# ConvFFN of a two-layer backbone: partial sums of the seven products kept in PSUM, copied out by ScalarE

## The chip, the core and the metric

The kernel runs on one core of a Trainium2 chip. Its engines have queues of their own: TensorE (PE in the profile, its weight loads PEld), VectorE (DVE), ScalarE (ACT), GpSimd (POOL) and SyncE (SP), which here issues nearly all DMAs. The metric is the device time of one execution in microseconds (us).

## The reference, cut to what matters

Two layers work on 1024 latent tokens of width 1024; the first also updates 256 context tokens. Both layers end in this feed-forward network, in float32:

```python
def conv_ffn(h, w_up, conv_w, conv_b, w_down):      # D_FF = 2816
    a = h @ w_up                                    # (L, 1024) @ (1024, 5632)
    gate, val = a[..., :D_FF], a[..., D_FF:]
    gp = jnp.pad(gate, ((0, 0), (1, 1), (0, 0)))
    g = gp[:, 0:L] * conv_w[0] + gp[:, 1:1 + L] * conv_w[1] + gp[:, 2:2 + L] * conv_w[2] + conv_b
    return (jax.nn.silu(g) * val) @ w_down
...
x = x + g2 * conv_ffn(modulate(x, norm2_g[layer], sh2, sc2), ...)
```

## The kernel before

Everything is transposed: channels lie on the 128 partitions, tokens along the free dimension. A float32 product is made of three TensorE passes over high and low parts (`PASSES`); `split` (L445) makes the parts, the high one with a copy on ACT (L447), the low one with a subtraction on DVE or POOL (L448).

The tokens are worked in two halves, one after the other (`s` = 0, 1), and D_FF in 22 blocks of 128 channels (`f`). A step `up(s, f, ...)` computes the gate and the value of one block for one half. The half's tokens are cut once more into two pieces of n columns, and the 1024 input channels into two parts, so that a step is a 2x2 by 2x2 block product; it is done with seven block products `P1` to `P7` in place of eight (`PROD`), each 12 matmuls of n columns into one PSUM bank. n is 320 and 324 in layer 0 (latents and context), 256 and 258 in layer 1. The results are `c00`, `c01` (the gate's two pieces) and `c10`, `c11` (the value's), in one SBUF tile `hx`:

- `c00` = P1 + P2, `c01` = P1 + P6 + P5 + P3,
- `c10` = P1 + P6 + P7 + P4, `c11` = P1 + P6 + P7 + P5.

Each product has a bank of its own (tag `pq`, eight buffers, all of PSUM). ACT copies P1 out (L323), and seven additions on DVE (`add`, L311) make the four sums. `gate` (L315 to L321) applies the convolution and the silu; L361 multiplies by the value, and a split makes the tile `act`, the moving operand of the down product.

Between the products of step f stand four calls of `down` (L368) for earlier blocks: two blocks' `act` by the weights `wd`, 6 matmuls into a bank (over all 2n columns at n = 256, else two banks of n columns), which a DVE instruction adds to the stream `xl` (L382). A step has 84 matmuls of products and 48 of n columns of `down` (24 of 512 columns at n = 256).

A step's weights are seven operands. Two loads of 512 KB, SP's `load0` (gate columns, tile `wr`, halves A00 and A01) and `load1` (value columns, A10 and A11), are combined on POOL: S1 = A10 + A11 (L241), S3 = A00 - A10 (L247, over A10), S2 = S1 - A00 (L248, over A00), S4 = A01 - S2 (L251, over S1). Each of A00, S2, S1, S4 (tiles `wh`), A01, S3, A11 (`wq`) is then split into its slot, which can be written when PE has done the product that uses it: A00 by P1, A01 by P2, S2 by P6, S1 by P5, S3 by P7, A11 by P4, S4 by P3. In most steps POOL makes the low parts of A00, A01 and A11, DVE the others. There are two `wr` buffers, so the next `load0` waits until S2 is split and S4 made, the next `load1` until S3 and A11 are split. All of this runs two steps ahead of the products.

`ORDER` is the order in which a step's products are written; `FEED` says after which product which weight is split, `AFTER` after which product how many `down` calls stand; `todo` lists the additions with the products that each needs. The order that the engines really get is set by a scheduler when the program is built; instructions written under `high_priority` are preferred by it.

Of the kernel before, what the change touches and what calls it, by code (L numbers as in the profile page):

```python
# [11 lines left out]
AF = mybir.ActivationFunctionType  # L12
# [3 lines left out]
P = 128  # L16
# [62 lines left out]
class Ffn:  # L79
# [10 lines left out]
                P6=("S2", "T2"), P7=("S3", "T3"))  # L90
# [1 line left out]

    ORDER = ("P1", "P2", "P6", "P5", "P7", "P4", "P3")
    FEED = dict(P2=("A00",), P6=("A01",), P5=("S2",), P7=("S1", "load0"), P4=("S3", "A11", "load1"), P3=("S4", "s"))
    AFTER = dict(P5=1, P4=1, P3=2)
    AFTER2 = dict(P4=1, P3=3)

    ORDER0 = ("P1", "P2", "P3", "P5", "P6", "P7", "P4")
# [175 lines left out]
    def up(self, s, f, hooks, downs, prep, beside):  # L274

        nc, net = self.nc, self.net
        h = self.halves[s]
        n = h.n
        g0 = s * NF + f
        self.busy = len(downs) > 0  # L280
        if g0 == 0:
            now, w = self.first
            self.slots["A11"] = self.t([P, 2, 4, P], "wq", F32R, 3)
            self.soon = self.up_weights(1, self.slots)
            self.soon["load0"]()
        else:
            w = self.slots
        soon = self.soon if g0 + 1 < 2 * NF else {}
        steps = dict(soon) if g0 + 1 < 2 * NF else {}
        for x in ("load0", "load1", "s"):  # L290
            steps.pop(x, None)
        if g0 + 2 < 2 * NF:
            self.soon = self.up_weights((f + 2) % NF, self.slots)
            steps.update((x, self.soon[x]) for x in ("load0", "load1", "s"))
        gv = net.t(net.hpool, [P, net.width], "hx", bufs=2)
        C0, C1 = gv[:, :2 * n], gv[:, self.w2:self.w2 + 2 * n]
        c00, c01, c10, c11 = C0[:, :n], C0[:, n:], C1[:, :n], C1[:, n:]
        cw, layer = net.convw[self.layer], self.layer
        g = self.t([P, self.w2], "g", bufs=1)[:, :2 * n]

        def product(p):
            wn, bn = self.PROD[p]
            o = net.t(net.ps, [P, 512], "pq" if p in ("P2", "P5") else "pq")[:, :n]
            for k in range(4):
                for i, (wp, sp) in enumerate(PASSES):
                    nc.tensor.matmul(o, w[wn][:, wp, k], self.part(s, bn, k, sp), start=(k == 0 and i == 0),  # L306
                                     stop=(k == 3 and i == 2))
            return o

        def add(o, x, y):  # L310
            nc.vector.tensor_tensor(o, x, y, ALU.add)  # L311

        def gate():
            w0, w1, w2 = (cw[:, j * NF + f:j * NF + f + 1] for j in range(3))
            nc.scalar.activation(g, C0, AF.Identity, bias=net.convb[:, layer * NF + f:layer * NF + f + 1], scale=w1)  # L315
            for _, _, m, c in h.span:
                nc.vector.scalar_tensor_tensor(g[:, c + 1:c + m], C0[:, c:c + m - 1], w0, g[:, c + 1:c + m],
                                               ALU.mult, ALU.add)
                nc.vector.scalar_tensor_tensor(g[:, c:c + m - 1], C0[:, c + 1:c + m], w2, g[:, c:c + m - 1],
                                               ALU.mult, ALU.add)  # L320
            nc.scalar.activation(g, g, AF.Silu)  # L321
        x = {}
        todo = [("P1", lambda: nc.scalar.activation(c00, x["P1"], AF.Copy)),  # L323
                ("P1 P6", lambda: add(c10, x["P6"], c00)),
                ("P6 P2", lambda: add(c00, c00, x["P2"])),
                ("P6 P5", lambda: add(c01, x["P5"], c10)),
                ("P6 P5 P7", lambda: add(c10, c10, x["P7"])),
                ("P6 P5 P7", lambda: add(c11, c10, x["P5"])),
                ("P6 P5 P7 P4", lambda: add(c10, c10, x["P4"])),
                ("P6 P5 P3", lambda: add(c01, c01, x["P3"])),  # L330
                ("P6 P5 P3 P2", gate)]
        order, feed = (self.ORDER if f else self.ORDER0, self.FEED if f >= 2 - s else (self.FEED0, self.FEED1)[f])
        cut = 3 - f if f < 2 and s == 0 else 7
        for i, p in enumerate(order):
            if i == cut:
                yield
            x[p] = product(p)
            if g0 == i == 0:
                w["A11"] = self.t([P, 2, 4, P], "wd", F32R, 4)
                for st in (now["A11"], soon["load1"], soon["s"]):  # L340
                    st()
            if i in hooks:
                hooks[i]()
            if i == 2:
                prep()
            if i in beside:
                beside[i]()
            for it in [it for it in todo if set(it[0].split()) <= set(x)]:
                todo.remove(it)
                with net.tc.high_priority():  # L350
                    it[1]()
            m = (self.AFTER if f != 2 else self.AFTER2).get(p, 0)
            for fn in downs[:m]:
                fn()
            downs = downs[m:]
            for st in feed.get(p, ()):
                if st in steps:
                    steps[st]()
        act = self.acts[f] = self.act()
        with net.tc.high_priority():  # L360
            nc.vector.tensor_tensor(g, g, C1, ALU.mult)  # L361
            self.tail = net.split(act[:, 0, :2 * h.n], act[:, 1, :2 * h.n], g)
# [66 lines left out]
class Net:  # L429
# [487 lines left out]
    def fourier(self, fl, fc, tables, pool):  # L917
# [876 lines left out]
```

## Time and profile before

| | |
|---|---|
| time, median of 3 runs | 2914.47 us (2912.04 to 2919.38) |
| the profiled execution | 2920.99 us; its span, from the first to the last instruction, 2919.1 us |
| busy, share of the span | PE 95%, PEld 86%, DVE 76%, ACT 45%, POOL 43% |
| feed-forward network of layer 0 | about 486 to 1440 us of the span |
| feed-forward network of layer 1 | about 2137 to 2919 us |
| products (L306) and down products (L376) | 7392 and 3696 matmuls |
| additions (L311) | 616 |

Times in the profile are from the start of the span. A busy share is an average over stages with different limits, so the two networks, and the two halves in each, are read apart. A group of the profile is the instructions of one line, engine and operation with equal tile names: its count, its busy time, the mean duration of one in ns, and behind the second bar the engine's idle time just before them with what ended it.

### The profile page before, as it was taken

Reading aid. Unit: us, or ns where it says so; the run is one execution under the profiler, and the core shown is the slowest. Engines: PE = TensorE matmul, PEld = TensorE weight load, DVE = VectorE, ACT = ScalarE, POOL = GpSimd, SP = SyncE. Lnnn points to the kernel's source line nnn. Section 1 sums busy time; section 2 is a strip of 40 time slices with the busy share of each in tenths; the row PEclk is TensorE's granted clock in tenths of the full one; section 3 lists DMA queues with packets and bytes.
Section 4 is the critical chain, followed back from the end, with each engine's and each line's share of the span. In section 5 each row is a group of like instructions: output and inputs, shape, how many; then the busy total and the mean of one; then the engine's idle time right before and its main releaser. Section 6 shows DMA issues by size and latency. Waiting matters only on the chain.

```text
span 2919.1 us, 47590 instructions
## 1 busy us (share of the span) xinstructions
PE 2772.8 (95%) x17978; PEld 2522.4 (86%) x17978; DVE 2216.9 (76%) x3748; ACT 1302.0 (45%) x2448; POOL 1267.9 (43%) x1044
## 2 busy tenths in 40 slices
PE   7999998899999999999999998999989999899998
PEld 4668877799999899999888888998778888799998
DVE  4243477999989999998767668996498777887786
ACT  4221314434444443443443336996354444444443
POOL 0600025455555755553311112443455665666663
PEclk9999999899999999999899999999989999999999
DMA  8663262322223222222052327772133323333323
GB/s 303 215 189 118 98 217 72 112 74 86 80 87 101 75 80 87 73 81 87 24 169 101 137 109 183 180 179 80 37 109 101 95 87 98 105 89 93 94 88 95
DMA packets 335886, 327.67 MB, mean 112 GB/s; under 512 B 16217, under 2 KB 264617, under 8 KB 335657
## 3 DMA queue, kind: packets, MB, share of 16 engines
q1 hardware_dynamic: 331509, 315.69, 35.9%
q0 software_dynamic: 3808, 7.87, 0.9%
q8 instruction: 143, 2.34, 0.3%
q10 hardware_dynamic: 340, 1.06, 0.1%
q14 instruction: 86, 0.70, 0.1%
HBM read 277.86 MB, written 46.71 MB: 111 GB/s over the span
## 4 chain that ended last, share of the span: by engine, by line
PE 61%; DVE 14%; DMA 7%; POOL 7%; issue 5%; ACT 5%; SPq 0%; POOLq 0%; DVEq 0%; ACTq 0%
PE pq L306 18%; PE pq L478 15%; PE pq L376 11%; PE ps L478 6%; DMA wr<-in_ffn_w_up_dram 4%; POOL ws L241 2%; DVE xl L382 2%; DVE wh L448 2%; PE pq L566 2%; POOL wh L448 2%; DVE hx L311 2%; PE ps L487 2%; ACT t L1227 1%; POOL wr L248 1%; DMA wd<-in_ada_w_dram 1%
## 5 line engine op out<-in xcount | busy, mean ns | idle before, releaser
L376 PE MATMUL pq<-act,wd 128*128 128x320 f32 (+3 forms) x3696 | 639.8, 322 | 59.3 <-DVE xl L382 24.5
L376 PEld LDWEIGHTS pq<-act,wd 128*128 128x128 f32 x3696 | 557.1, 193 | 92.0 <-DVE xl L382 28.7
L306 PE MATMUL pq<-hs,wh 128*128 128x320 f32 (+3 forms) x4128 | 607.5, 299 | 16.3 <-DVE xl L382 7.8
L306 PEld LDWEIGHTS pq<-hs,wh 128*128 128x128 f32 x4128 | 576.9, 191 | 26.4 <-DVE xl L382 11.2
L306 PE MATMUL pq<-hs,wq 128*128 128x320 f32 (+3 forms) x3144 | 469.8, 299 | 8.4 <-DVE wq L448 4.9
L478 PE MATMUL pq<-hs,wh 128*128 128x512 f32 (+3 forms) x2100 | 469.0, 358 | 3.6 <-DVE hs L724 1.9
L306 PEld LDWEIGHTS pq<-hs,wq 128*128 128x128 f32 x3144 | 442.5, 191 | 14.1 <-DVE wq L448 5.7
L478 PEld LDWEIGHTS pq<-hs,wh 128*128 128x128 f32 x2100 | 365.8, 193 | 78.0 <-issue 6.2
L241 POOL TENSOR_TENSOR ws<-wr 128x512 f32<-128x512 f32 x88 | 153.6, 1745 | 397.3 <-DMA wr<-in_ffn_w_up_dram 333.0
L447 ACT ACTIVATE wh<-wr 128x512 fp32r<-128x512 f32 (+1 forms) x223 | 161.8, 726 | 354.0 <-POOL wr L248 201.5
L382 DVE SCALAR_TENSOR_TENSOR xl<-pq,mod,xl 128x320 f32<-128x320 f32 (+5 forms) x616 | 304.1, 514 | 11.7 <-PE pq L376 11.6
L448 DVE TENSOR_TENSOR wh<-wr,wh 128x512 fp32r<-128x512 f32 (+1 forms) x147 | 166.9, 1135 | 184.8 <-ACT wh L447 184.5
L448 POOL TENSOR_TENSOR wq<-wr,wq 128x512 fp32r<-128x512 f32 x152 | 235.7, 1550 | 32.9 <-ACT wq L447 32.9
L478 PE MATMUL ps<-hs,wh 128*128 128x512 f32 x840 | 240.0, 405 | 3.6 <-ACT hs L721 1.8
L311 DVE TENSOR_TENSOR hx<-hx,pq 128x320 f32<-128x320 f32 (+3 forms) x440 | 196.1, 448 | 29.1 <-PE pq L306 21.6
L447 ACT ACTIVATE wq<-wr 128x512 fp32r<-128x512 f32 x262 | 160.0, 623 | 101.3 <-PE pq L306 73.2
L447 ACT ACTIVATE wh<-ws 128x512 fp32r<-128x512 f32 x172 | 107.5, 625 | 169.8 <-PE pq L306 115.4
L478 PEld LDWEIGHTS ps<-hs,wh 128*128 128x128 f32 x840 | 141.9, 191 | 41.6 <-issue 14.4
L251 POOL TENSOR_TENSOR ws<-wr 128x512 f32<-128x512 f32 x88 | 120.2, 1366 | 123.3 <-DVE wh L448 112.3
L999 POOL TENSOR_TENSOR hsp<-hsq,hsp 128x512 fp32r<-128x512 f32 (+1 forms) x40 | 47.1, 1185 | 265.5 <-ACT hsq L998 265.5
L1006 DVE RECIPROCAL hsq<-hsq 128x512 f32<-128x512 f32 (+1 forms) x40 | 121.1, 3030 | 52.9 <-ACT hsq L1005 52.1
L448 DVE TENSOR_TENSOR wd<-wrd,wd 128x512 fp32r<-128x512 f32 x176 | 155.5, 912 | 0.2 <-ACT wd L447 0.2
(310 smaller groups left out, 4555.5 us busy)
## 6 DMA issues: line engine op xcount, KB each, us to landing
wr<-in_ffn_w_up_dram SPq DMA_DIRECT2D x176, 512.0 KB, 4.4
wrd<-in_ffn_w_down_dram SPq DMA_DIRECT2D x88, 512.0 KB, 3.5
adaw<-in_ada_w_dram SPq DMA_DIRECT2D x128, 256.0 KB, 3.6
wd<-in_ada_w_dram SPq DMA_DIRECT2D x32, 512.0 KB, 5.1
wr<-in_odd_w_qkv_dram SPq DMA_DIRECT2D x24, 512.0 KB, 3.9
vd<-kvs SPq DMA_DIRECT2D x8, 1280.0 KB
v<-vd SPq DMA_DIRECT2D x16, 640.0 KB
kd<-kvs SPq DMA_DIRECT2D x8, 1280.0 KB, 4.6
```

What stands on the lines that cost most here:

```text
L241: op(raw["S1"], raw["A10"], raw["A11"], ALU.add)
L251: op(x, raw["A01"], raw["S2"], ALU.subtract)
L306: nc.tensor.matmul(o, w[wn][:, wp, k], self.part(s, bn, k, sp), start=(k == 0 and i == 0), stop=(k == 3 and i == 2))
L311: nc.vector.tensor_tensor(o, x, y, ALU.add)
L376: nc.tensor.matmul(pd, self.wds[j][i][:, wp, d % 4], self.acts[f][:, sp, lo:lo + m], start=(i == 0 and pi == 0), stop=(i == len(fs) - 1 an ...
L382: nc.vector.scalar_tensor_tensor(x, pd[:, a - lo:b - lo], net.mod[:, self.layer, st, 5, d:d + 1], x, ALU.mult, ALU.add)
L447: self.nc.scalar.activation(h, src, AF.Copy)
L448: return (e or self.nc.vector).tensor_tensor(l, src, f32(h), ALU.subtract)
L478: nc.tensor.matmul(o, w(wp, k), s(k, sp), start=(ki == 0 and pi == 0), stop=(ki == len(order) - 1 and pi == 2))
L487: nc.tensor.matmul(out, l[a], r[b], start=(first and i == 0), stop=(last and i == 2))
L566: nc.tensor.matmul(acc[32 * q:32 * q + 32, 0:256], self.sT[:, k, :], w[q // 2][:, 256 * (q % 2):256 * (q % 2) + 256], start=(k == 0), stop ...
L1006: nc.vector.reciprocal(r, r)
```

## The change

In all steps but f = 0, P6 is accumulated into the bank of P1, P7 further into the same bank, and P3 into the bank of P5; in steps 3 to 20 (`last`) P4 goes into the first bank as well. Between the products ACT copies the bank's state to SBUF: after P1 (`c00`), after P6 (`c01`), after P7 (`c10`), and in steps 3 to 20 after P4 (`c10` again). DVE keeps the additions of P2 to `c00`, of P5 to make `c11`, and of the second bank to `c01`. A step 3 to 20 thus has four copies and three additions in place of one and seven, and uses three banks for its products in place of seven. A product that adds to a bank can't start before the bank has been copied out, and P3 not before the addition that reads P5. One `down` call moves from behind P5 to behind P7 (`AFTER`).

```diff
-    AFTER = dict(P5=1, P4=1, P3=2)
+    AFTER = dict(P7=1, P4=1, P3=2)
...
-            o = net.t(net.ps, [P, 512], "pq" if p in ("P2", "P5") else "pq")[:, :n]
+            o = net.t(net.ps, [P, 512], "pq")[:, :n] if p not in onto else x[onto[p]]
             for k in range(4):
                 for i, (wp, sp) in enumerate(PASSES):
-                    nc.tensor.matmul(o, w[wn][:, wp, k], self.part(s, bn, k, sp), start=(k == 0 and i == 0),
-                                     stop=(k == 3 and i == 2))
+                    nc.tensor.matmul(o, w[wn][:, wp, k], self.part(s, bn, k, sp),
+                                     start=(p not in onto and k == 0 and i == 0),
+                                     stop=(k == 3 and i == 2), skip_group_check=p in onto)
...
+        def copy(o, x):
+            nc.scalar.activation(o, x, AF.Copy)
+        x, onto = {}, {}
+        last = f > 2 and len(downs) > 0
+        if f == 0:
...
+        else:
+            onto = dict(P6="P1", P7="P6", P3="P5")
+            if last:
+                onto["P4"] = "P7"
+            todo = [("P1", lambda: copy(c00, x["P1"])),
+                    ("P2", lambda: add(c00, c00, x["P2"])),
+                    ("P6", lambda: copy(c01, x["P6"])),
+                    ("P7", lambda: copy(c10, x["P7"])),
+                    ("P7", lambda: add(c11, c10, x["P5"])),
+                    ("P4", lambda: copy(c10, x["P4"]) if last else add(c10, c10, x["P4"])),
+                    ("P3", lambda: add(c01, c01, x["P3"])),
+                    ("P3", gate)]
```

Outside the two networks the order of instructions stays as it was. Inside, the scheduler moves more than the additions. (In the new program the copies are L325, the splits L466 and L467, the silu L323, the gate L317; L236, L241, L247, L248, L251, L261 keep their numbers. Numbers behind tile names count buffers.)

ACT in a step of layer 1's second half, before: the high parts of A00, then the copy of P1, the silu, A01, `act`, S1, S2, S3, A11, S4, and the next gate.

```order
L447 ACTIVATE wh_20746<-wr_27112 128x512 [waits DMAHW1_49,PE_49]
L323 ACTIVATE hx_27208<-pq_27210 128x258 [waits PE_49]
L321 ACTIVATE g_27005<-g_27005 128x516 [waits DVE_49,Activation_49]
L447 ACTIVATE wq_20648<-wr_27112 128x512 [waits PE_49]
L447 ACTIVATE act_27204<-g_27005 128x516 [waits DVE_49]
L447 ACTIVATE wh_20747<-ws_27202 128x512 [waits PE_49,Pool_49]
L447 ACTIVATE wh_20746<-wr_27112 128x512 [waits Pool_49]
L447 ACTIVATE wq_20649<-wr_27148 128x512 [waits DMAHW2_49,PE_49]
L447 ACTIVATE wq_20973<-wr_27148 128x512 [waits PE_49]
L447 ACTIVATE wh_20747<-ws_27202 128x512 [waits PE_49,Pool_49]
L315 ACTIVATE g_27209<-hx_27208,cols_31_139,cols_175_786 128x516 [waits DVE_49,Activation_49]
```

The same place now, from S1 on: S1, `act`, the copy of P6, S2 (which waits for POOL's L248), S3, the copy of P7, two splits of `wd`, A11, the copy of P4, S4.

```order
L466 ACTIVATE wh_20543<-ws_27440 128x512 [waits PE_49,Pool_49]
L466 ACTIVATE act_27442<-g_27248 128x516 [waits DVE_49]
L325 ACTIVATE hx_27446<-pq_27448 128x258 [waits PE_49]
L466 ACTIVATE wh_20542<-wr_27352 128x512 [waits Pool_49]
L466 ACTIVATE wq_20445<-wr_27387 128x512 [waits DMAHW3_49,PE_49]
L325 ACTIVATE hx_27446<-pq_27448 128x258 [waits PE_49]
L466 ACTIVATE wd_27691<-wrd_27498 128x512 [waits DMAHW4_49,PE_49]
L466 ACTIVATE wd_27694<-wrd_27498 128x512 [waits PE_49]
L466 ACTIVATE wq_20769<-wr_27387 128x512 [waits PE_49]
L325 ACTIVATE hx_27446<-pq_27448 128x258 [waits DVE_49,PE_49]
L466 ACTIVATE wh_20543<-ws_27440 128x512 [waits PE_49,Pool_49]
```

The copies of P6 and P7 stand behind splits that wait for POOL, and P7 and P4 on PE wait for them; A11 now stands behind P4, which PE reaches only after the copy of P7.

POOL in one step of layer 1's first half, before: S1, S3, the low part of A00, S2, that of A01, S4, that of A11.

```order
L241 TENSOR_TENSOR ws_22846<-wr_22808 128x512 [waits DMAHW1_49,DVE_49]
L247 TENSOR_TENSOR wr_22808<-wr_22780,wr_22808 128x512 [waits DMAHW0_49,Pool_49]
L448 TENSOR_TENSOR wh_20746<-wr_22780,wh_20746 128x512 [waits PE_49,Activation_49]
L248 TENSOR_TENSOR wr_22780<-ws_22846,wr_22780 128x512 [waits Pool_49]
L448 TENSOR_TENSOR wq_20648<-wr_22780,wq_20648 128x512 [waits PE_49,Activation_49]
L251 TENSOR_TENSOR ws_22846<-wr_22780 128x512 [waits DVE_49,Pool_49]
L448 TENSOR_TENSOR wq_20973<-wr_22808,wq_20973 128x512 [waits PE_49,Activation_49]
```

Now the steps go in pairs. From the end of one step's combining through the other's:

```order
L251 TENSOR_TENSOR ws_22761<-wr_22724 128x512 [waits DVE_49,Pool_49]
L467 TENSOR_TENSOR wh_20542<-wr_22864,wh_20542 128x512 [waits DMAHW6_49,PE_49,Activation_49]
L467 TENSOR_TENSOR wq_20444<-wr_22864,wq_20444 128x512 [waits PE_49,Activation_49]
L467 TENSOR_TENSOR wq_20769<-wr_22724,wq_20769 128x512 [waits PE_49,Activation_49]
L241 TENSOR_TENSOR ws_22928<-wr_22891 128x512 [waits DMAHW0_49,DVE_49]
L247 TENSOR_TENSOR wr_22891<-wr_22864,wr_22891 128x512 [waits Pool_49]
L248 TENSOR_TENSOR wr_22864<-ws_22928,wr_22864 128x512 [waits Pool_49]
L251 TENSOR_TENSOR ws_22928<-wr_22891 128x512 [waits DVE_49,Pool_49]
L467 TENSOR_TENSOR wq_20769<-wr_22891,wq_20769 128x512 [waits PE_49,Activation_49]
L467 TENSOR_TENSOR wh_20542<-wr_23031,wh_20542 128x512 [waits DMAHW1_49,PE_49,Activation_49]
L467 TENSOR_TENSOR wq_20444<-wr_23031,wq_20444 128x512 [waits PE_49,Activation_49]
```

A00 and A01 of the next step (from the tile that its `load0` fills) are now split before L241, while `load1` is awaited; in one step of a pair A11 stands in front of them, in the other behind them. In layer 1's second half, and in layer 0's, one step of a pair has A00 and A01 ahead of L241 and the other has one or both between L241 and L248, as before.

SP in the same half, before: `load0`, `load1` one behind the other, then the load of a `wd` pair (`wrd`).

```order
L236 DMA wr_22780<-in_ffn_w_up_dram 128x8x128 [waits DMAHW5_49,Pool_49]
L236 DMA wr_22808<-in_ffn_w_up_dram 128x8x128 [waits DMAHW6_49,DVE_49,Pool_49]
L261 DMA wrd_22904<-in_ffn_w_down_dram 128x2x512 [waits DMAHW7_49,DVE_49]
L236 DMA wr_22952<-in_ffn_w_up_dram 128x8x128 [waits DMAHW0_49,Pool_49]
L236 DMA wr_22980<-in_ffn_w_up_dram 128x8x128 [waits DMAHW1_49,DVE_49,Pool_49]
L261 DMA wrd_23076<-in_ffn_w_down_dram 128x2x512 [waits DMAHW2_49,DVE_49]
```

Now:

```order
L236 DMA wr_22864<-in_ffn_w_up_dram 128x8x128 [waits DMAHW3_49,DVE_49,Pool_49]
L261 DMA wrd_22986<-in_ffn_w_down_dram 128x2x512 [waits DMAHW4_49,DVE_49]
L236 DMA wr_22891<-in_ffn_w_up_dram 128x8x128 [waits DMAHW5_49,Pool_49]
L236 DMA wr_23031<-in_ffn_w_up_dram 128x8x128 [waits DMAHW6_49,DVE_49,Pool_49]
L261 DMA wrd_23153<-in_ffn_w_down_dram 128x2x512 [waits DMAHW7_49,DVE_49]
L236 DMA wr_23058<-in_ffn_w_up_dram 128x8x128 [waits DMAHW0_49,Pool_49]
```

`load0` goes out as soon as S2 is split; `load1` waits for A11 on POOL alone, and the load of `wrd` stands between the two. On PE a step's order is now P1, P2, P5, P6, P7, P4, P3 (before: P1, P2, P6, P5, P7, P4, P3), with `down` matmuls before P6, around P7, and the next P1 begun before P4.

More of the change, by code (lines that the diff above doesn't have):

```diff
@@ L321, in gate @@
             nc.scalar.activation(g, g, AF.Silu)
[L322 to L331, printed above, removed]
+        def copy(o, x):
[4 more added lines that the diff above has]
+            todo = [("P1", lambda: copy(c00, x["P1"])),
+                    ("P1 P6", lambda: add(c10, x["P6"], c00)),
+                    ("P6 P2", lambda: add(c00, c00, x["P2"])),
+                    ("P6 P5", lambda: add(c01, x["P5"], c10)),
+                    ("P6 P5 P7", lambda: add(c10, c10, x["P7"])),
+                    ("P6 P5 P7", lambda: add(c11, c10, x["P5"])),
+                    ("P6 P5 P7 P4", lambda: add(c10, c10, x["P4"])),
+                    ("P6 P5 P3", lambda: add(c01, c01, x["P3"])),
+                    ("P6 P5 P3 P2", gate)]
+        else:
+            onto = dict(P6="P1", P7="P6", P3="P5")
+            if last:
+                onto["P4"] = "P7"
+            todo = [("P1", lambda: copy(c00, x["P1"])),
+                    ("P2", lambda: add(c00, c00, x["P2"])),
[5 more added lines that the diff above has]
+                    ("P3", gate)]
         order, feed = (self.ORDER if f else self.ORDER0, self.FEED if f >= 2 - s else (self.FEED0, self.FEED1)[f])
```

## The prediction

> **What bounds the kernel now.** I read the page's head first, then the engines' busy time by stage, then one row of each stage that gives the length of a step, and last PE's waits and the chain of waits in the stages where PE stands idle.
>
> ```profile
> span 2919.1 us, 47590 instructions
> ...
> PE 2772.8 (95%) x17978; PEld 2522.4 (86%) x17978; DVE 2216.9 (76%) x3748; ACT 1302.0 (45%) x2448; POOL 1267.9 (43%) x1044
> ```
>
> The profiled execution took 2920.99 us, 1.9 more than its span and 6.5 more than the median of the three runs, 2914.47. The sum below is a difference, which I subtract from both. All of it must come out of PE's idle time, 146.3 us, since the change keeps every matmul. The busy time by stage shows where that idle time lies (rows: stretch, its length, then busy time of PE, PEld, DVE, ACT and POOL, granted clock, DMA share, GB/s; the first two lie in layer 0, halves 1 and 2, the next two in layer 1, the last two are the whole networks):
>
> ```profile
> 718.10:911.30 193.20, 193.20 (x1317) 193.20 (x1316) 174.49 (x311) 80.64 (x130) 109.67 (x70) 1.00 0.27 82
> 1066.90:1343.70 276.80, 276.42 (x1850) 273.99 (x1849) 253.21 (x435) 112.90 (x182) 149.52 (x98) 1.00 0.27 81
> 2241.20:2479.20 238.00, 226.01 (x1544) 208.00 (x1543) 181.99 (x295) 102.41 (x183) 142.97 (x98) 0.99 0.31 94
> 2593.80:2859.80 266.00, 247.12 (x1993) 244.84 (x1992) 201.34 (x376) 110.16 (x196) 170.75 (x105) 0.98 0.31 92
> 486.00:1440.00 954.00, 919.31 (x6005) 900.76 (x6004) 876.89 (x1511) 416.99 (x716) 517.02 (x357) 0.97 0.27 80
> 2137.00:2919.10 782.10, 719.82 (x5248) 680.90 (x5246) 613.30 (x1038) 340.34 (x615) 461.95 (x310) 0.97 0.32 97
> ```
>
> In layer 0 PE is never idle (193.20 of 193.20, 276.42 of 276.80), though DVE is busy 90%. In layer 1 DVE is busy only 76% and PE idles 12.0 us of the third stretch and 18.9 of the fourth. The gate's first ACT instruction comes once a step, so its count and first and last start give the steps:
>
> ```profile
> L315 ACT ACTIVATE g<-hx,cols,cols x15: 929/931/933, 1066.9 to 1343.7; 128x648 f32<-128x648 f32 x15
> ...
> L315 ACT ACTIVATE g<-hx,cols,cols x15: 814/817/821, 2241.2 to 2479.2; 128x512 f32<-128x512 f32 x15
> ...
> L315 ACT ACTIVATE g<-hx,cols,cols x16: 817/820/823, 2593.8 to 2859.8; 128x516 f32<-128x516 f32 x16
> ```
>
> Layer 0, half 2: 276.8 / 14 = 19.77 us, all of it PE. Layer 1, half 1: 238.0 / 14 = 17.00, of which PE needs 226.01 / 14 = 16.14; half 2: 266.0 / 15 = 17.73, of which 247.12 / 15 = 16.47. A step can't become shorter than those. What PE waits for in half 2, and in half 1:
>
> ```profile
> PE pq L376 <- DVE xl L382: 18.9, 11, 2.3
> ...
> PE pq L376 <- ACT act L447: 6.7, 5, 2.2
> ```
>
> All the idle time of half 2 ends with a DVE addition into `xl`, which frees a PSUM bank. That addition is only the last link; the chain of waits, over one step of half 2 (start, length, what), shows what came before it:
>
> ```profile
> 2659.09 0.64 ACT wh L447
> ...
> 2660.87 0.86 DVE xl L382 x2
> 2661.74 0.33 DVE hx L311
> 2662.07 0.61 DVE wq L448
> ...
> 2662.74 5.15 DMA wr<-in_ffn_w_up_dram
> ...
> 2668.03 3.09 POOL ws L241
> ...
> 2672.79 1.74 POOL wh L448
> ...
> 2675.74 1.29 POOL wr L248
> ...
> 2677.05 0.64 ACT wh L447
> ```
>
> It is a ring: S2's high part on ACT (2659.09), on DVE the rest with S3's low part (2662.07), then `load1` goes out, lands after 5.15 us, S1 on POOL, A00's low part, S2, and S2's high part again at 2677.05, 17.96 us later, a step. No PE is in it. While DVE waits for S2's high part, its `xl` additions stand behind, and PE runs out of banks. Half 1 has the same ring with one more POOL piece:
>
> ```profile
> 2319.38 0.64 ACT wh L447
> ...
> 2320.05 1.10 DVE wh L448
> ...
> 2322.23 1.28 POOL ws L251
> 2323.51 1.78 POOL wq L448
> 2325.30 4.88 DMA wr<-in_ffn_w_up_dram
> ...
> 2330.32 1.82 POOL ws L241
> ...
> 2336.50 0.64 ACT wh L447
> ```
>
> **The change, part by part.** Additions and copies first (minimum, median, maximum in ns):
>
> ```profile
> L311 DVE TENSOR_TENSOR hx<-hx,pq x440: 401/448/494, 516.8 to 2889.2; 128x320 f32<-128x320 f32 x37, 128x324 f32<-128x324 f32 x37, 128x258 f32<-128x258 f32 x37, 128x256 f32<-128x256 f32 x36
> ...
> L323 ACT ACTIVATE hx<-pq x88: 357/400/423, 489.5 to 2880.5; 128x320 f32<-128x320 f32 x22, 128x324 f32<-128x324 f32 x22, 128x256 f32<-128x256 f32 x22, 128x258 f32<-128x258 f32 x22
> ```
>
> A middle step loses four additions, 4 x 0.45 = 1.8 us of DVE, and gains three copies, 3 x 0.40 = 1.2 us of ACT; 324 and 240 over the run. In layer 0 the 1.8 us lie beside a PE that never waits, so they are worth nothing; in layer 1 the ring holds one addition (0.33 us), which leaves. ACT, busy 41% in half 2 (110.16 / 266), has room for the copies. What can cost is the waiting for them: P6 may not start before P1's copy, P7 before P6's, P4 before P7's. A matmul takes 19.77 / 132 = 0.15 us in layer 0 (84 product and 48 `down` matmuls a step), and between P6 and P7, and P7 and P4, stand about 12 `down` matmuls, 1.8 us, against a 0.40 us copy: 1.4 us in hand. It goes when the copy stands behind S2's split, which waits for POOL, and POOL here works 149.52 / 14 = 10.7 of 19.77 us, so it is seldom that late. I take +3 us for layer 0's 36 middle steps: bounds 0 (copies always covered) and +12 (a third of a microsecond in each; a gain is excluded by PE's full rows).
>
> For layer 1 the terms are the ring's own pieces, by shape over half 2 and, in the last two rows, half 1 (count, busy us, mean ns, idle before):
>
> ```profile
> L241 POOL TENSOR_TENSOR ws<-wr 128x512 f32<-128x512 f32 x15 | 43.6, 2904 | 83.2 <-DMA wr<-in_ffn_w_up_dram 71.9 <-DVE xl L382 5.7 <-DVE g L319 5.7
> L448 POOL TENSOR_TENSOR wq<-wr,wq 128x512 fp32r<-128x512 f32 x30 | 39.5, 1315 | 5.9 <-ACT wq L447 5.9
> L448 POOL TENSOR_TENSOR wh<-wr,wh 128x512 fp32r<-128x512 f32 x15 | 26.1, 1738 | 0.0
> L247 POOL TENSOR_TENSOR wr<-wr,wr 128x512 f32<-128x512 f32 x15 | 24.5, 1631 | 1.2
> ...
> L448 DVE TENSOR_TENSOR act<-g,act 128x516 fp32r<-128x516 f32 x15 | 14.8, 987 | 4.7 <-ACT act L447 4.7
> L447 ACT ACTIVATE act<-g 128x516 fp32r<-128x516 f32 x15 | 9.5, 636 | 11.7 <-DVE g L361 11.7
> ...
> L448 POOL TENSOR_TENSOR wh<-wr,wh 128x512 fp32r<-128x512 f32 x14 | 21.6, 1543 | 0.0
> L241 POOL TENSOR_TENSOR ws<-wr 128x512 f32<-128x512 f32 x14 | 21.2, 1517 | 69.7 <-DMA wr<-in_ffn_w_up_dram 60.3 <-DVE wd L448 4.7 <-DVE g L319 4.7
> ```
>
> L241 waits for the load 71.9 us of half 2, 4.8 a step: `load1`'s landing is the ring's longest piece. A load that flies alone lands sooner:
>
> ```profile
> wr<-in_ffn_w_up_dram SPq DMA_DIRECT2D x1, 512.0 KB, 3.7
> ```
>
> That is one that goes out first of its pair. The change now lets the loads go out one behind the other, and it moves POOL and SP: A00 and A01 of the next step are split while `load1` flies, but A11 stands behind P4 or behind them. So the steps go in pairs, which I sum link by link, with landings of 3.7 alone and 4.9 (the 4.88 above) behind another transfer.
>
> Half 2, the step with A00 and A01 inside the ring: L241 2.90, A00 1.74, L247 1.63, A01 1.32, S2 1.29 (8.88); S2's and S3's splits and P7's copy 1.6 (the chain's 0.64, 0.61 and 0.40); P4, 12 of 132 matmuls of 16.47, 1.5, since A11 waits for it; A11's high part 0.64 and low part 1.32; hand-overs 0.5; `load1` behind `wrd` 4.9: 19.3. The other: L241 2.90, S1's split 0.64, P4 and a `down` call before it 3.0, `act`'s high part 0.64 and low part 0.99 between, A11 1.96, hand-overs 0.4, `load1` alone 3.7: 14.2. The pair is 33.5, against 35.46 before; nine pairs: 9 x -1.9 = -17 us. With every landing at 3.7 it is 32.3, below PE's 32.94, so PE sets it: -23. With 4.9 everywhere 34.7: -7.
>
> Half 1, one step: L241 1.52, L247 1.62 (its half 2 row is 1.63), S2 1.28; S2's split 0.64 and 1.1; `load0` 3.7; A00's high part 0.64; A00, A01 and A11 on POOL, 3 x 1.54 = 4.6; `load1` 3.7; hand-overs 0.5: 19.3. The other, where A11 is early and `load1` lands beside the rest: 4.4 + 1.7 + 3.7 + 0.64 + 2 x 1.54 + 0.4 = 13.9. The pair is 33.2, against 34.0; nine pairs -7; I take -5, since hand-overs show in the chain only where they were the last. Bounds: PE's 32.28, so -15; with all three landings at 4.9, 36.8, so +25. This is the term that can turn: the ring now holds two loads in one step, where it had one.
>
> Stage ends: of PE's 62.3 idle us in layer 1 (782.10 - 719.82), some 31 lie outside the middle steps; the first and last steps keep P4's bank and lose three additions. I put 0, between -10 and +5. Outside both networks instructions keep their order: 0.
>
> Sum: +3 - 17 - 5 + 0 = -19: 2920.99 becomes 2902, and 2914.5 becomes **2895 us**.
>
> One rule of the Trainium skill would raise the gain. Its page "SBUF — State Buffer", section "SBUF: two separate sides", says that DVE and GpSimd share a port pair that is held for a whole instruction, by a DVE operation with two SBUF inputs among others, not by one with an input in PSUM. By that rule the removed additions, which read PSUM, free POOL of nothing, and the 1.8 us give no second gain; the rows above agree only so far that the same L241 took 1.52 us in half 1 and 2.90 in half 2, with the additions in both. What it would make of L241 in the new order is the third rival.
>
> **The rivals.**
> - *The loads chain (slower).* If in half 1 the loads, one behind another and with `wrd` between, land at 4.9, the pair is 36.8, +25 us; half 2 then gains only 7 and layer 0 costs 3: +21, **2935 us**. For it: the 4.88 and 5.15 us of the chains. Against: in the new order `load0` and `load1` are over 5 us apart. It decides from a mean landing of 3.7 + 0.8 / 3 = 4.0 us on.
> - *The ring keeps its length (no change).* PE has banks to spare, but the copies of P6 and P7 stand on ACT behind splits that wait for POOL's S2, so PE waits for copies in place of banks; half 2 gains only the 0.33 us addition, 18 x -0.33 = -6, and layer 0's +3 to +6 takes it: **2914 us**. For it: the chain has PE in no link, so more banks alone shorten nothing. Against: the landing of 5.15 falls in the other order.
> - *L241 gets quick (more).* If L241 in half 2 no longer meets a slow neighbour and takes 1.52, its pair is 33.5 - 2 x 1.38 = 30.7, and PE's floor holds: 18 x (16.47 - 17.73) = -23; half 1 at its floor -15; ends -10: -48, **2866 us**. Against: the DVE work of two SBUF inputs (splits, the multiplication into `act`) all stays.
>
> **How the numbers follow.** Forecast 0.45 (its own range 2880 to 2905), loads chain 0.23, ring keeps 0.20, L241 quick 0.12. About 0.3%, 9 us, is what a measurement of this kernel can tell from no change. So faster 0.57, same 0.20, slower 0.23. The range runs from 2866, the floor, to 2935; I leave about 0.2 outside, half of the two outer cases.
>
> **What would show it.** In the changed profile the gate's ACT row gives the steps: half 1 near 16.7, half 2 near 16.8, layer 0 19.8 to 19.9 us. L241 should wait under 4 us a step for its load, POOL's rows in pairs. PE's waits should no longer name `xl`; if they name the `hx` copies on ACT for over 10 us a half, the second rival is right. Landing of `wr` loads above 4.2 with half 1 above 17.5 us shows the first; L241 below 2 us in half 2 the third. PE idle in layer 0 above 15 us would break the first term. I would be wrong most easily on half 1, where two loads in one step leave 0.4 us a step.

## The result: 3.2% slower, and the profile after

The changed kernel takes 3007.49 us (median of 4 runs, 3002.23 to 3009.74) against 2914.39 for the kernel before in the same comparison: a ratio of 1.0315, with a 95% interval of 1.0296 to 1.0334. The forecast was 2895, the range ended at 2935. The page's head and busy line:

```profile
span 3000.5 us, 47161 instructions
...
PE 2792.7 (93%) x17978; PEld 2530.1 (84%) x17978; DVE 2199.4 (73%) x3424; ACT 1376.2 (46%) x2688; POOL 1235.2 (41%) x1044
```

The counts are those announced: 324 DVE instructions fewer, 240 ACT instructions more, PE's the same. DVE is busy only 17.5 us less, though 324 additions of 0.45 us are 146 us: its other instructions together took some 128 us longer. The span is 81.4 us longer. Where it went is in the windows from the gate of step 4 to that of step 20, 16 steps (layer 0 halves 1 and 2, layer 1 halves 1 and 2; columns as before):

```profile
603.90:931.30 327.40, 314.16 (x2114) 310.25 (x2113) 261.10 (x433) 141.69 (x257) 165.38 (x112) 1.00 0.26 76
1074.50:1410.80 336.30, 321.12 (x2114) 318.01 (x2113) 265.26 (x432) 144.85 (x258) 168.05 (x112) 0.98 0.25 76
2256.10:2552.00 295.90, 266.16 (x1747) 240.25 (x1746) 243.38 (x279) 131.77 (x260) 169.60 (x112) 0.97 0.29 88
2670.40:2955.00 284.60, 264.38 (x2104) 259.84 (x2104) 229.80 (x337) 132.93 (x257) 164.91 (x112) 0.98 0.30 89
```

A sixteenth of each length is the step. Layer 0, which had no idle time on PE, now has 13.2 and 15.2 us of it in 16 steps; DVE fell from 90% to 80%. The step lengths of all runs, taken in the same way between the gates of steps 4 and 20:

| us per step | layer 0, half 1 | half 2 | layer 1, half 1 | half 2 | time, us |
|---|---|---|---|---|---|
| before | 19.47 | 19.73 | 17.13 | 17.74 | 2914.4 |
| changed | 20.46 | 21.02 | 18.49 | 17.79 | 3007.5 |
| e1 S1 behind `act` | 20.92 | 21.11 | 18.11 | 17.09 | 2995.8 |
| e2 `AFTER` undone | 20.53 | 20.60 | 18.55 | 17.68 | 2995.5 |
| e3 `AFTER` alone | 19.38 | 19.59 | 17.51 | 18.01 | 2920.7 |
| e4 P4 apart | 20.83 | 20.69 | 17.12 | 17.47 | 2971.1 |
| e5 downs behind products | 25.04 | 25.40 | 20.38 | 20.22 | 3230.9 |
| e6 downs spread | 19.73 | 19.96 | 17.74 | 18.20 | 2968.7 |
| e7 e6 with P4 apart | 19.74 | 19.99 | 17.99 | 18.29 | 2972.6 |
| e8 before, less cover | 20.21 | 21.34 | 17.13 | 17.18 | 2944.0 |
| e9 middle steps only | 21.04 | 20.94 | 18.36 | 17.70 | 2985.0 |
| e10 layer 1 only | 19.38 | 19.81 | 17.26 | 17.18 | 2914.2 |
| e11 before, layer 1's calls moved | 19.52 | 19.73 | 17.08 | 17.19 | 2909.0 |

The middle steps (18 in a half), taken at these lengths, lose 18 x (0.99 + 1.29 + 1.36 + 0.05) = 66 us; the other 15 us of the span lie in the first and last steps. PE's waits in these windows of the changed kernel, in layer 0's half 2, layer 1's half 1 and its half 2 (us in all, times, longest):

```profile
PE pq L395 <- ACT act L466: 15.1, 8, 2.4
...
PE pq L307 <- ACT hx L325: 21.5, 16, 2.1
...
PE pq L395 <- DVE act L467: 11.2, 8, 1.4
PE pq L395 <- ACT act L466: 7.9, 8, 1.6
```

No wait is put down to `xl` any more, as forecast; but PE waits for `act` in layer 0 and in half 2 of layer 1 (every other step), and for the copies in half 1. One such wait in layer 0, from the last addition of the step to PE (timeline: start, length, engine, line, what):

```profile
784.53 0.47 DVE L313 TENSOR_TENSOR hx<-hx,pq 128x320 f32<-128x320 f32 x1
785.03 0.93 ACT L317 ACTIVATE g<-hx,cols,cols 128x640 f32<-128x640 f32 x1
...
790.06 0.83 DVE L380 TENSOR_TENSOR g<-g,hx 128x640 f32<-128x640 f32 x1 [0.47 <-ACT g L323]
790.87 1.29 POOL L241 TENSOR_TENSOR ws<-wr 128x512 f32<-128x512 f32 x1 [2.75 <-DMA wr<-in_ffn_w_up_dram]
...
792.19 0.63 ACT L466 ACTIVATE wh<-ws 128x512 fp32r<-128x512 f32 x1 [2.16 <-POOL ws L241]
792.73 0.72 ACT L466 ACTIVATE act<-g 128x640 fp32r<-128x640 f32 x1
...
793.88 1.90 DVE L467 TENSOR_TENSOR act<-g,act 128x640 fp32r<-128x640 f32 x1
795.84 0.41 PE L395 MATMUL pq<-act,wd 128*128 128x320 f32 x1 [1.19 <-DVE act L467]
```

`act` could have been split at 790.9, when L380 ended, but ACT stood at S1's split, which waits for POOL's L241, which waits for the load. That was the obvious culprit, and the first theory (A). Moving it away did not shorten layer 0's steps.

### The profile page after: what moved, and what is told of

Read it like the earlier page. It is cut to its first block, busy times and chain, and to the rows that moved or that the text cites. A ratio compares the mean times of both kernels' runs of the same rounds, so it can differ in the third digit from the quotient of the medians.

```text
span 3000.5 us, 47161 instructions
## 1 busy us (share of the span) xinstructions
PE 2792.7 (93%) x17978; PEld 2530.1 (84%) x17978; DVE 2199.4 (73%) x3424; ACT 1376.2 (46%) x2688; POOL 1235.2 (41%) x1044
## 3 DMA queue, kind: packets, MB, share of 16 engines
q10 hardware_dynamic: 340, 1.06, 0.1%
## 4 chain that ended last, share of the span: by engine, by line
PE 48%; DVE 19%; DMA 13%; POOL 7%; ACT 7%; issue 5%; SPq 0%; POOLq 0%; ACTq 0%; DVEq 0%
PE pq L497 14%; PE pq L307 11%; DMA wr<-in_ffn_w_up_dram 10%; PE pq L395 8%; PE ps L497 6%; DVE wh L467 3%; DVE xl L401 3%; DVE wd L467 2%; POOL ws L241 2%; ACT t L1246 2%; POOL wq L467 2%; PE pq L585 2%; PE ps L506 1%; DVE g L380 1%; ACT wh L466 1%
## 5 line engine op out<-in xcount | busy, mean ns | idle before, releaser
L307 PE MATMUL pq<-hs,wh 128*128 128x320 f32 (+3 forms) x4128 | 621.7, 300 | 20.0 <-ACT hx L325 5.6
L307 PE MATMUL pq<-hs,wq 128*128 128x320 f32 (+3 forms) x3144 | 483.4, 302 | 36.9 <-ACT hx L325 29.2
L467 POOL TENSOR_TENSOR wq<-wr,wq 128x512 fp32r<-128x512 f32 x152 | 220.6, 1453 | 271.3 <-ACT wq L466 256.8
L466 ACT ACTIVATE wh<-wr 128x512 fp32r<-128x512 f32 (+1 forms) x223 | 162.3, 728 | 315.8 <-DMA wr<-in_ffn_w_up_dram 96.8
L467 DVE TENSOR_TENSOR wh<-ws,wh 128x512 fp32r<-128x512 f32 x172 | 180.9, 1051 | 116.7 <-ACT wh L466 110.3
L466 ACT ACTIVATE wq<-wr 128x512 fp32r<-128x512 f32 x262 | 163.0, 625 | 199.6 <-PE pq L307 159.4
L467 DVE TENSOR_TENSOR wh<-wr,wh 128x512 fp32r<-128x512 f32 (+1 forms) x147 | 171.1, 1164 | 90.5 <-ACT wh L466 90.1
L241 POOL TENSOR_TENSOR ws<-wr 128x512 f32<-128x512 f32 x88 | 125.7, 1429 | 241.2 <-DMA wr<-in_ffn_w_up_dram 195.7
L466 ACT ACTIVATE wh<-ws 128x512 fp32r<-128x512 f32 x172 | 108.0, 628 | 197.7 <-POOL ws L241 126.7
L467 POOL TENSOR_TENSOR wh<-wr,wh 128x512 fp32r<-128x512 f32 x76 | 107.7, 1417 | 184.3 <-ACT wh L466 177.0
L467 DVE TENSOR_TENSOR wd<-wrd,wd 128x512 fp32r<-128x512 f32 x176 | 158.6, 932 | 9.9 <-ACT wd L466 9.9
L313 DVE TENSOR_TENSOR hx<-hx,pq 128x320 f32<-128x320 f32 (+3 forms) x284 | 125.5, 446 | 54.5 <-PE pq L307 40.9
```

Source lines behind the costliest of these rows:

```text
L241: op(raw["S1"], raw["A10"], raw["A11"], ALU.add)
L466: self.nc.scalar.activation(h, src, AF.Copy)
L467: return (e or self.nc.vector).tensor_tensor(l, src, f32(h), ALU.subtract)
```

## The experiments

**e1: S1's split behind `act`.**

```diff
+            with ExitStack() as st:
+                if name == "S1" and getattr(self, "tail", None) is not None:
+                    st.enter_context(net.tc.issue_after(self.head.ins))
+                    st.enter_context(net.tc.issue_after(self.tail.ins))
+                net.split(slots[name][:, 0], slots[name][:, 1], x, ...)
```

`head` and `tail` are the ACT and the DVE instruction of the last split of `act`; the block's instructions are queued behind them.

> The changed kernel, with one order forced: on ACT and on DVE the split of S1 stands behind the split of act of the step, as it did before the change (no wait is added, the two only change places in the queue). Theory A (the queue order): the time is lost because S1's split, which waits for load1 and POOL's L241, now stands ahead of act, and PE's down product waits for act. Then layer 0 gets its steps of 19.4 and 19.8 us back (43 us), layer 1's half 2 loses its waits for act (some 10 us), half 1 stays at 18.4 us a step: 2945 to 2965 us. Theory B (the accumulation itself: P6, P7, P4 in a row on one bank, each behind a copy): the steps stay near 20.6, 21.0 and 18.4, the time stays over 2990 us.

2995.8 us, 1.0277 of before (1.0251 to 1.0302). Theory A holds in layer 1's half 2 (17.79 to 17.09, PE no longer waits for `act`) and falls in layer 0, where the steps stay at 20.9 and 21.1. The wait only changed its name there (layer 0, half 2):

```profile
PE pq L400 <- DVE xl L406: 13.0, 7, 2.3
```

`act` now comes in time: in most of the steps in which PE had waited for it, its high part is there 7.0 us after the last addition, in place of 8.6 in half 1 and 10 to 11 in half 2. PE stops a little later for a bank, since DVE stands at S2's split, which waits for the weights. So the lateness of `act` is not the only thing that holds layer 0's steps at this length.

**e2 and e3: the moved `down` call by itself.** e2 is the changed kernel with `AFTER = dict(P5=1, P4=1, P3=2)`, e3 the kernel before with `AFTER = dict(P7=1, P4=1, P3=2)`.

> The changed kernel with the down call put back behind P5 (AFTER as before). Theory C (the moved down call brings act's first use too early on PE, or leaves P6 without cover): layer 0 goes back to its old steps, 2950 us or less. Theory A: S1's split stays ahead of act on ACT in most steps, so layer 0 stays near 20.6 to 21 us a step: 2990 to 3015 us. Theory B: 2990 us or more too.

> The kernel before with nothing but the moved down call (behind P7 in place of P5), no accumulation. Theory A: act stays ahead of S1 on ACT, so 2905 to 2925 us, no change. Theory C: over 2950 us.

e2 takes 2995.5 us, 1.0273 (1.0243 to 1.0302), e3 2920.7 us, 1.001 (0.9994 to 1.0025). The moved call is not the cause: alone it does nothing that can be measured, and taken back it returns 12 us of 93.

**e4: P4 in a bank of its own.**

```diff
-        last = f > 2 and len(downs) > 0
+        last = False
```

> The changed kernel with P4 in a bank of its own and added by DVE in every step (the accumulation of P6, P7 and P3 stays). Theory A: S1's split still stands ahead of act, but A11 no longer waits behind P4 behind P7's copy, so load1 goes out earlier and the wait for act shrinks by half: layer 0 near 20.0 us a step, the time 2950 to 2985 us. Theory B: one link in three of the serial sums goes: 2975 to 2985 us, with PE's waits named by the hx copies, and not by act.

2971.1 us, 1.0205 (1.0169 to 1.0242). The time lies in theory A's range and 4 us below theory B's, but the steps fit neither: layer 0 stays at 20.8 and 20.7 us, where A had 20.0, and PE's waits there still name `act`, which B excluded. Layer 1's half 1 is back at its old 17.12 us: its whole loss came with P4 in the first bank. There A11 could be split only after P4, which waited for P7's copy, and so `load1` went late: the loads of `wr` make up 25.9% of the chain of waits of this stage in the changed kernel, 6.3% in e4. PE's own waits for the copies (21.5 us above) go as well, to 1.7 (it waits 12.9 for DVE's additions there), so e4 doesn't tell how the loss divides between the two.

So I counted, in PE's order, the matmuls between P3's end and the first that needs the new `act`. Before the change there are 78: two `down` calls behind P3 (24), P1, P2, P6 and P5 (48), and 6 of the older block. In the changed kernel the scheduler, with P4 held for a copy and P3 for an addition, had put those `down` calls ahead of P4 and P3; I counted 62 that are left. That holds for the step shown above; in the trace, in the eight steps of each half in which PE then waits, 59 are left in half 2, and 54 in seven of half 1's eight. At 0.147 us that is 11.5 us of cover against 8.7 and 7.9 (9.1 in the step shown). The chain from the last addition to `act`'s low part, in the kernel before:

```profile
1106.14 0.49 DVE L311 TENSOR_TENSOR hx<-hx,pq 128x324 f32<-128x324 f32 x1 [0.18 <-PE pq L306]
...
1116.79 0.75 ACT L447 ACTIVATE act<-g 128x648 fp32r<-128x648 f32 x1 [3.02 <-DVE g L361]
1117.57 1.03 DVE L448 TENSOR_TENSOR act<-g,act 128x648 fp32r<-128x648 f32 x1 [0.81 <-ACT act L447]
1117.59 0.30 PEld L376 LDWEIGHTS pq<-act,wd 128*128 128x128 f32 x2 [0.16 <-ACT act L447]
```

That is 12.5 us (the high part is there at 11.4), longer than the 11.25 of the changed kernel above, and PE hardly waited for it: the last line is the first weight load that needs the new `act`, 0.16 us late. The cover had shrunk, not the chain grown: theory D.

**e5 and e6: the `down` calls held behind their product.**

```diff
+            with ExitStack() as st:
+                if f > 2 and m:
+                    st.enter_context(net.tc.issue_after(self.mm.ins))
                 for fn in downs[:m]:
                     fn()
```

`mm` is the product's last matmul. e6 also has `AFTER = dict(P6=1, P7=1, P3=2)`.

> The changed kernel with one order forced, on PE alone: the down calls that are written behind P7, P4 and P3 stay behind that product's last matmul (they had moved ahead of P4 and P3, which the scheduler held back for P7's copy). Theory D (the cover of the gate): between P3's end and the first down matmul that needs the new act, PE had 78 matmuls before the change (11.5 us in layer 0) and 62 in the changed kernel (9.1 us), while gate, silu, product and split take 11 us; the weight work fell into pairs for the same reason. With the downs back behind P3 there are 87, so the waits for act go and the weights go step by step again; left over is a wait of 0.6 us a step, since P7 now follows P6 with only the copy between: 20.1 and 20.4 us a step in layer 0, 2920 to 2945 us. Theory B (accumulation itself): over 2980 us. Theory A2 (the weights' ring in pairs, which comes from A11 behind P4): layer 0 unchanged at 20.5 to 21, over 2975 us.

> As e5, and the down calls put where the copies need cover: one behind P6, one behind P7, two behind P3, none behind P4. Theory D: each copy has 12 down matmuls beside it (1.8 us in layer 0), so 19.5 to 19.8 us a step in layer 0 and 16.5 to 17.5 in layer 1: 2885 to 2915 us. Theory B: over 2980 us.

e5 missed, 286 us above theory D's range: 3230.9, 1.109 (1.1064 to 1.1115). With nothing between P6 and P7, P6's copy lies bare on PE's path, and on ACT it stands behind the splits of S1 and S2. One wait, in layer 0's half 2:

```profile
1235.21 1.71 POOL L248 TENSOR_TENSOR wr<-ws,wr 128x512 f32<-128x512 f32 x1
1236.95 0.63 ACT L469 ACTIVATE wh<-wr 128x512 fp32r<-128x512 f32 x1 [3.38 <-POOL wr L248]
1237.48 0.42 ACT L325 ACTIVATE hx<-pq 128x324 f32<-128x324 f32 x1
...
1237.96 3.61 PE L307 MATMUL pq<-hs,wq 128*128 128x324 f32 x12 [3.74 <-ACT hx L325]
```

A copy of 0.42 us cost PE 3.74, the time in which ACT waited for POOL's S2. Idle time is not all of it. Over half 2's middle steps the granted clock is 0.90, against 1.00 in the kernel before, and the falls lie where such waits end:

```profile
1236.48:1243.29 6.81, 5.33 (x20) 5.33 (x21) 1.96 (x3) 1.92 (x4) 1.71 (x2) 0.50 0.26 77
```

A step there is 5.67 us longer than before the change and PE's idle time 3.64; the slower clock goes with most of the rest. So e5 did not separate the theories; e6 did, with a `down` call of 12 matmuls behind P6 and one behind P7, and in layer 0 P6's copy ahead of S2's split on ACT. It takes 2968.7 us, 1.0184 (1.0163 to 1.0204), 54 us over theory D's range, but not for the sake of layer 0's middle steps: there, with every accumulation kept, the steps are 19.73 and 19.96 us, 0.73 and 1.06 less than in the changed kernel, and PE is busy again (half 2; length, then PE):

```profile
1057.60:1377.00 319.40, 317.81 (x2114) 313.28 (x2113) 270.36 (x432) 144.98 (x258) 165.02 (x112) 1.00 0.26 80
```

The steps are within 0.26 and 0.23 us of the kernel before. So layer 0 lost by where the `down` calls stood, and not by the accumulation as such (theory B); nor by A11 behind P4 (theory A2), since P4 is still in the first bank. But e6 restores two things at once: the cover (in the step whose gate starts at 1197.57 us, 78 matmuls again), and the order of the weight work (between 720 and 757 us POOL splits A00 behind L241 in both steps, where the changed kernel splits it ahead), with steps of even length: about 19.6 and 19.8 us in turn in half 1, in place of mostly 19.0 and 22.2. Theory D named both, cover and weights; since e1 met the weights as soon as `act` was early, e6 doesn't say what each is worth.

Two things I missed. The profiled run is 48 us longer than that of the kernel before, and the middle steps, by the table, make 28 of them. In the other steps the gate of step 21 stands out: it comes 4 to 6 us later after that of step 20 in each of the four halves, 21 us in all; step 21 has no `down` calls. And in layer 1 e6's middle steps are slower than before (19 of the 28 us), with PE waiting for copies in half 2, and a new ring in the chain of waits:

```profile
PE pq L307 <- ACT hx L325: 22.5, 16, 1.7
```

```profile
2717.90 0.64 ACT wq L469
...
2718.61 1.30 POOL wq L470
...
2719.93 3.69 DMA wr<-in_ffn_w_up_dram
...
2723.75 2.57 POOL ws L241
...
2731.00 1.70 POOL wr L248
...
2733.88 0.28 ACT hx L325
...
2734.20 1.60 PE pq L307 x11
...
2735.83 0.64 ACT wq L469
```

The ring that had no PE in it now runs through PE: A11's split, `load1`, S1, S2, then P7's copy behind S2's split on ACT, then P4, whose end frees A11's slot: 17.9 us from one A11 to the next.

**e7: e6 with P4 apart** (`last = False`).

> As e6, with P4 in a bank of its own and added by DVE in every step. Theory D: the same time as e6 within 10 us in layer 0; in layer 1 A11 no longer waits for P7's copy, so the same or up to 10 us less than e6: 2880 to 2915 us. Theory B: between e6 and the kernel before.

2972.6 us, 1.02 (1.0181 to 1.0218), 58 us over the range: layer 0 as e6, layer 1 no better (17.99 and 18.29). With P4 out of the bank PE waits for DVE's additions instead (20.4 us in half 2's 16 steps), so the accumulation of P4 was not the only link there. Which of the remaining ones sets these steps I have not separated.

**e8: the kernel before, with less cover.** `AFTER = dict(P5=1, P7=1, P4=2)`, nothing else.

> The kernel before, no accumulation, with the two down calls from behind P3 put behind P4, and the one behind P4 behind P7: 65 matmuls stand between P3 and the first use of the new act, in place of 78. Theory D: layer 0's steps grow by 0.5 to 1.2 us as in the changed kernel, with PE waiting for act: 2935 to 2975 us. Theory B (it takes the accumulation): 2905 to 2925 us.

2944.0 us, 1.0103 (1.0079 to 1.0127), in theory D's range. Without any accumulation layer 0 loses 0.74 and 1.61 us a step, and PE waits for the same thing, 19.9 us in 16 steps of half 2. Half 2 loses more than the 1.2 that I had allowed, because less cover is left than I had counted: in the trace 51 matmuls, not 65, in each step in which PE waits (61 in most of half 1's). 51 x 0.147 = 7.5 us against 9.9 to `act`'s high part leaves 2.4 us, and the longest wait is 2.5:

```profile
PE pq L376 <- ACT act L447: 19.9, 8, 2.5
```

From the last addition of such a step on, the chain of waits has the gate and nothing of the weights:

```profile
1212.34 0.94 ACT g L315
1213.30 2.78 DVE g L317 x2
1216.08 3.02 DVE g L319 x2
1219.18 0.75 ACT g L321
1219.96 0.96 DVE g L361
1220.94 0.75 ACT act L447
1221.73 0.56 PE pq L376 x2
```

So lost cover alone, without the accumulation, costs layer 0 as much as the change did. e8 also gained where I had not looked: layer 1's half 2 went from 17.74 to 17.18.

**e9: accumulation in steps 3 to 20 alone** (`if f == 0:` becomes `if not last:`).

> The changed kernel with the accumulation in steps 3 to 20 alone; steps 1, 2 and 21 add up with DVE as before the change. In the changed kernel the time outside the middle steps grew too, by 10 us in layer 0 and 13 in layer 1. Theory E (those steps lose by the accumulation in themselves, with no down calls to cover the copies): 20 us come back, 2980 to 2992 us, the middle steps unchanged. Rival (those are late after-effects of the middle steps, or of the moved down call): 3000 us or more.

2985.0 us, 1.0239 (1.0222 to 1.0256): 22 us less than the changed kernel, as theory E said, though its middle steps are some 5 us longer in all (18 x 0.28). Adding up in the bank costs in the first and last steps themselves.

**e10 and e11: is there a version that is faster than both?** e10 accumulates in layer 1's middle steps only, P4 apart, with e1's order; e11 is the kernel before with e8's `AFTER` in layer 1 only. This is e11's edit:

```diff
+    AFTERX = dict(P5=1, P7=1, P4=2)
...
-            m = (self.AFTER if f != 2 else self.AFTER2).get(p, 0)
+            m = ((self.AFTERX if len(self.xs) == 1 else self.AFTER) if f != 2 else self.AFTER2).get(p, 0)
```

> Layer 0 as before the change; in layer 1, steps 3 to 20, the accumulation of P6, P7 and P3 with P4 in a bank of its own, and S1's split behind act on ACT and DVE as in e1. By the steps of e4 (17.1 in half 1) and e1 (17.1 in half 2) and no loss at the ends: 0 and 18 x -0.65 = -12 us against the kernel before, 2896 to 2910 us. If the gains of e1 and e4 don't add: 2910 to 2925 us.

> The kernel before without accumulation; in layer 1 alone the two down calls from behind P3 stand behind P4 and the one behind P4 behind P7 (what e8 did in both layers, where layer 1's network took 9 us less). Expected 2900 to 2910 us. If that gain was chance or came with layer 0's delay: 2911 to 2920 us.

e10: 2914.2 us against 2916.1, 0.9992 (0.9983 to 1.0001), no difference, and in the second of its ranges; half 2 gains 0.56 us a step, half 1 gives 0.13 back, and the rest is lost outside them. e11: 2909.0 us, 0.9979 (0.9968 to 0.999), the fastest of all, without an accumulated product, but by 0.2% only, less than the 0.3% that the prediction took as the least that tells: three `down` calls in another place shorten half 2 as much as the accumulation with e1's order does. In both, the granted clock of half 2 is higher too (0.99 and 1.00, against 0.98 in the kernel before), so the 0.56 us are not all waiting.

## Why the prediction was wrong

- **Layer 0, +3 (0 to +12): it was +41** (18 x 0.99 + 18 x 1.29). This is the step that failed. I asked what stood between the products that now wait for copies (12 `down` matmuls for each, right) and took "PE never waits" as slack. But those matmuls were taken from somewhere: from behind P3, where they had covered the gate. 78 matmuls against a chain of 11 to 12 us had been just enough. The busy table doesn't show that, but in the kernel before the waits of the weight loads hint at it: in 16 steps of layer 0's half 2 they wait 7 times for `act`'s low part, up to 0.2 us each.

```profile
PEld pq L376 <- DVE act L448: 1.2, 7, 0.2
```

  e6 gives most of the loss back by placing calls, e8 makes one like it without the change; how it divides between cover and weights stays open. The order lists showed the next P1 begun before P4 and `down` calls moved; I did not count what was left behind P3.
- **Layer 1, half 1, -5 (-15 to +25): it was +24** (18 x 1.36), at the upper bound. A pair takes 37.0 us where the first rival had 36.8. By the sign that I had set (landings above 4.2 with steps above 17.5) that rival would be shown: the loads of `wr` land after 4.8 us in the median. But they took 4.8 in the kernel before as well, and 4.4 in e4, where the steps are back at 17.12. The chain of waits, with the two ends of a pair:

```profile
2359.50 3.73 DMA wr<-in_ffn_w_up_dram
...
2393.84 1.77 DVE wd L467
2395.62 0.61 DVE wh L467
...
2396.28 3.75 DMA wr<-in_ffn_w_up_dram
...
2405.51 3.87 DMA wr<-in_ffn_w_up_dram
```

  Here the landings are 3.7 to 3.9 us, as I took them. What the sum left out is what stands in front: S2's low part came at 2395.62 behind a `wd` split of 1.77 us on DVE, and `load1` went out at 2382.78 right behind the load of `wrd`, 2.9 us after `load0`:

```profile
2379.87 0.37 SPq L236 DMA_DIRECT2D wr<-in_ffn_w_up_dram  x1
2382.32 0.37 SPq L261 DMA_DIRECT2D wrd<-in_ffn_w_down_dram  x1
2382.78 13.87 SPq L236 DMA_DIRECT2D wr<-in_ffn_w_up_dram  x2
```

  I had added links as if each began when its own input was there. e4 shows that the whole loss goes with P4's place behind P7's copy.
- **Layer 1, half 2, -17 (-23 to -7): it was +1.** L241 even took 1.37 us in place of 2.90, the third rival's condition, and its wait for the load fell from 71.9 to 36.8 us:

```profile
L241 POOL TENSOR_TENSOR ws<-wr 128x512 f32<-128x512 f32 x16 | 22.0, 1373 | 56.5 <-DMA wr<-in_ffn_w_up_dram 36.8 <-PE pq L307 14.6 <-DVE g L321 5.1
```

  The gain was given back at once: `act` stood behind S1's split. With the two exchanged (e1) it is -0.65 us a step, -12 us. I had seen S1 ahead of `act` in the order lists and put no price on it. The loads, too, took longer than in my sum: 4.8 to 6.6 us where they stand in the chain of this stage, against the 4.9 and 3.7 that I had put.
- **Stage ends, 0 (-10 to +5): about +15 in the span; e9, without the accumulation in those steps, is 22 us faster.** I costed three additions fewer and not the copies, which have few `down` calls or none beside them there.
- The signs set beforehand did not tell the rivals apart. PE's waits for the copies in layer 1's half 1 (21.5 us, the sign was 10) speak for the second, L241's 1.37 us for the third, the landings for the first; none of their three times came out, because none of them put more than 6 us on layer 0. Only the sign for the first term, PE idle in layer 0 above 15 us, pointed at the step that failed: it was 28 us in the 32 steps shown.
- The price of a bare copy, "when the copy stands behind S2's split", was named and called seldom. It was rare in layer 0 of the changed kernel; e5, where it happens in each step, shows it at 3.7 us.
- Of the two costs at nothing, the additions were indeed worth nothing: DVE at 80% in place of 90% made nothing in layer 0 faster.

The Trainium skill has a rule that spoke against the change, on its page "Perfetto Trace Analysis", section "Matmuls": independent groups should rotate through different PSUM banks, so that one's evacuation overlaps the next one's matmuls. Seven products in three banks, or four in steps 1, 2 and 21, give that up. e5 and e9 agree with it: with nothing beside it, PE waits 3.7 us for a copy of 0.42 that stands behind another split, and steps 1, 2 and 21, with few `down` calls or none beside the copies, cost 22 us. e6 shows its limit: in layer 0 the same three banks, with `down` calls beside the copies of P6 and P7, cost 0.26 and 0.23 us a step.

## What to carry to other kernels

When products are chained on one bank, each copy takes its cover from independent work, and that work was covering something else: count the matmuls ahead of every consumer on PE, before and after, and set them against the chain that they hide. A stage in which PE never waits may have no slack at all; short waits of its weight loads for one tile are a sign of that. An in-order engine that copies PSUM out must not have an instruction in front of the copy that waits for a load.

## What was unexpected of the hardware

- A wait on PE costs more than the idle time that the windows show. In layer 0's half 2 the step grew by 1.29 us and PE's idle time by 0.93 (0.95 against 0.02). Two things make up the rest. First, the matmul after the one that had waited starts 0.25 us behind it and not 0.147 (the following ones keep 0.147 again), and the idle time is counted only from where the last matmul before the wait ended, some 0.16 us after the next could have started (a matmul lasts 0.31 us in the profile, one starts each 0.147); in half 1, at a clock of 1.00 and with about one wait a step, the step grew by 0.27 us more than the idle time. Second, after three of half 2's eight waits, those that ended at 1104.44, 1312.75 and 1397.88, the granted clock stood at 0.50 for 3.4 us; two of these stretches:

```profile
1105.62:1109.02 3.40, 3.40 (x14) 3.40 (x14) 1.50 (x1) 0.53 (x1) 0.95 (x1) 0.50 0.12 36
1313.83:1317.23 3.40, 3.40 (x15) 3.40 (x14) 1.59 (x1) 0.35 (x1) 1.05 (x1) 0.50 0.10 27
```

  Half of three times 3.4 us is 0.32 us for each of the 16 steps. After five waits of 1.4 to 2.4 us in the same window the clock stayed at 1.00; what decides it these runs don't show.
- POOL's L241 in layer 1's half 2 took 2.90 us before and 1.37 after with the same operands. Before, 14 of 16 ran beside five or six DVE instructions, two splits of `wd` among them, and took 2.7 to 3.5 us; the other two, and all 16 after, ran beside three or fewer and took 1.3 to 1.6. No run changes that alone, so the cause is not shown. It was a link of the ring, yet the kernel got no faster by it until the next wait was moved.
